# A DeltaNet recurrence with block-diagonal operands, weight buffers taken in turn, and one transition that adds its first half on VectorE

## The chip, the cores and the metric

The kernel runs on one core of a Trainium2 chip. The metric is the device time of one execution in microseconds (us); the time given for a kernel is the median over several executions.

A core has a matrix engine (TensorE; in the profile PE for the matrix products and PEld for the loading of their weights), a vector engine (VectorE, DVE), an activation engine (ScalarE, ACT), GpSimd (POOL), SyncE (SP), which here only issues transfers, and DMA engines. The engines run their own instruction queues in order and wait for each other through semaphores. SBUF holds tiles of 128 partitions; matrix products land in PSUM, of which this kernel makes eight buffers of 128x512 fp32: four named `pb` and four named `pd`.

## The reference

The kernel computes one layer of an encoder on a sequence of 512 positions with 16 learned positions ahead of it (528 in all) and 1024 channels:

```
h = h + 0.5 * post(swiglu_1(pre(h)))
h = h +       post(mixer(pre(h)))
h = h + 0.5 * post(swiglu_2(pre(h)))
```

`pre` and `post` are RMS norms. The mixer sums three gated branches and projects the sum with `w_out`. The branch that matters here is a gated delta rule with four heads of 128 channels, run once forward and once backward over the sequence in chunks of 64 positions:

```
def step(S, xs):                          # one chunk of one head and direction
    attn_n, u_n, w_n, qd_n, kd_n, gl_n = xs
    v_new = u_n - w_n @ S
    o = qd_n @ S + attn_n @ v_new
    S = S * gl_n[..., None, None] + jnp.swapaxes(kd_n, -1, -2) @ v_new
    return S, o
```

`t` (the inverse of a triangular 64x64 matrix) is folded into `u` and `w`; in the kernel it is applied to the difference instead.

## The kernel before, in words

**Weights.** All large products are made in fp32 accuracy from fp32r pieces: every weight block of 128 columns is brought by a DMA into `ws` (or `wf` in the FFNs), cast to fp32r by ScalarE (`wh`), and VectorE subtracts the cast from the original (`wl`). Three products, `wh` with the high and the low part of the data and `wl` with the high part, make one result. `load()` (lines 230 to 241) does this for a unit of one block, `pair_load()` (line 595 on) for the FFNs, where four blocks give seven combined ones. `wh` and `wl` live in the pool `wp`, which has 5 buffers for each, so a cast waits until TensorE has read the last of the block whose buffer it takes.

**Stages.** FFN 1 (to about 365 us), the transition `edge()` to the mixer, the mixer (to about 890 us; the output projection `w_out` makes up its end), the second `edge()`, FFN 2 and the output. TensorE's instructions stand in the order of the program text. The instructions of the other engines are placed by a scheduler with priorities: `AHEAD` puts loads 150 steps forward, `URGENT` evictions 450.

**The recurrence.** `dn_core` is a generator, run twice (two heads each time, each with a forward and a backward chain). It runs as a side program: whenever TensorE has worked for about `SC` = 1.8 us by the kernel's own count, `tick()` puts the next small group of products between those of the projections. A step s of 8 has three such groups. In the first, `kq` meets the state `Sst` (line 1446), and VectorE makes `vp` from the result (line 1450). In the second, `Z` (it shares the buffer `EZ`, and the profile shows that name) meets `vp` (line 1462), and ScalarE scales the result by `beta` into a second `vp` (line 1465; `v1` in the text). In the third, the decayed keys (`kd`, in the profile `sub`) and `at` meet `v1` (lines 1470 and 1473), and VectorE updates the state and the output `O`. A chunk has 64 positions, so the four products of `Z` and of `at` are 64x64, in the upper or lower half of the 128 partitions: at each step the forward chain is in one half and the backward chain in the other. The last step has no state to update, so its third group has `at` alone. An fp32 product shows as two PE records.

**The transitions.** In `edge()`, the last products of the stage before are accumulated for m = 0 to 7 in two halves of the columns. In the first edge, the sum of the earlier chunks (`y`) is copied into PSUM by ScalarE ahead of the products (line 355), which then add to it; the result is squared for the norm (lines 337 and 340) and copied back into `y` (line 343). VectorE sums the squares in `acc` (line 341). TensorE sums `acc` over the partitions (`stat`), and from the root VectorE and ScalarE make the new `h` and its pieces `x` block by block (`step`, lines 414 to 421), for which the first products of the next stage wait. In the second edge, the last three blocks of `w_out` make the tail, and the first blocks of FFN 2's weights are loaded.

Of the kernel before, what the change touches and what calls it, by code (L numbers as in the profile page):

```python
# [8 lines left out]
F32 = mybir.dt.float32  # L9
# [150 lines left out]
class K:  # L160
    def __init__(self, tc, A, ctx):
        self.tc, self.nc, self.A = tc, tc.nc, A
        self.n = 0
        self.sides = []
        self.T = Tensor(tc.nc)
# [4 lines left out]
        self.wp = e(tc.tile_pool(name="wp", bufs=5))  # L170
# [58 lines left out]
    def load(self, src, nk=KD, to=None):  # L229
# [100 lines left out]
    def leave_y(self, ya, m, ps, gain=None, table=KD - 2):  # L330
# [3 lines left out]
        for i, p in ps:  # L334
            w = acc[i].shape[1]
            if m == 0:
                ACT.activation(acc[i], p, AF.Square)
            else:
                sq = self.t(self.tp, "sy", [P, HN], F32, 1)[:, :w]
                ACT.activation(sq, p, AF.Square)  # L340
                V.tensor_tensor(acc[i], acc[i], sq, op=ALU.add)
            if gain is None:
# [19 lines left out]
    def start(self, xT, gpre, srcs):  # L362
# [8 lines left out]
               self.t(self.wp, "wl", [P, KD, P], F32R)) for i in range(len(srcs))]  # L371
        pieces = [slice(0, 1), slice(1, 2), slice(2, 4), slice(4, 6), slice(6, 8)]
# [30 lines left out]
    def edge(self, C, hT, ya, gpost, gpre, tail, switch, nxt, keep=None):  # L403
# [144 lines left out]
    def open_ffn(self):  # L548
        ctx = ExitStack()
        self.gp = ctx.enter_context(self.tc.tile_pool(name=self.uid("gp"), bufs=1))  # L550
        return ctx
# [44 lines left out]
    def pair_load(self, w1, w2):  # L596
# [4 lines left out]
        with self.tc.high_priority(AHEAD2):  # L601
# [7 lines left out]
            def put(f, a, b, w=KD, tag="w", pool=self.wp, bufs=None):  # L609
                h = self.t(pool, tag + "h", [P, w, P], F32R, bufs)  # L610
                l = self.t(pool, tag + "l", [P, w, P], F32R, bufs)
# [11 lines left out]
            put(fd, 4, None, 4, "w4", self.gp, 2)  # L623
# [242 lines left out]
    def mixer(self, pre, hT):  # L866
# [80 lines left out]
        def ready():  # L947
# [4 lines left out]
            mm = self.dctx.enter_context(self.tc.tile_pool(name="mm", bufs=1))  # L952
            return self.t(mm, "mh", [P, KD, S], F32R), self.t(mm, "ml", [P, KD, S], F32R)
# [13 lines left out]
        def tail():  # L967
            ws = [(m, self.load(A["wout"][m])) for m in range(KD - NT, KD)]
# [304 lines left out]
    def dn_core(self, st, slack):  # L1273
# [14 lines left out]
        at = self.t(dp, "at", B4)  # L1288
# [24 lines left out]
        for j in range(2):  # L1313
# [8 lines left out]
            for d in range(2):  # L1322
                V.tensor_tensor(A_[:, 2 * j + d], A_[:, 2 * j + d], b[:, :, 0], op=ALU.mult)
                V.tensor_tensor(at[:, 2 * j + d], E[:, 2 * j + d], b[:, :, 1], op=ALU.mult)
# [109 lines left out]
        yield SC  # L1434
        for s in range(8):
# [8 lines left out]
            vt = self.t(dp, "vp", [P, 4, P], F32, 2)  # L1444
# [3 lines left out]
            for j, d, hd, c, t, hf, X, Y, has in info:  # L1448
                if has:
                    V.scalar_tensor_tensor(vt[X, hd], b[X, hd * P:(hd + 1) * P], neg_eg[X, hd, t:t + 1], vn[X, j, t],  # L1450
                                           op0=ALU.mult, op1=ALU.add)
            for j, d, hd, c, t, hf, X, Y, has in info:
# [8 lines left out]
            for j, d, hd, c, t, hf, X, Y, has in info:  # L1461
                T.matmul(b[X, hd * P:(hd + 1) * P], Z[X, hd, t], vt[X, hd] if has else vn[X, j, t], start=True, stop=True)
            v1 = self.t(dp, "vp", [P, 4, P], F32, 2)
            for j, d, hd, c, t, hf, X, Y, has in info:
                ACT.activation(v1[X, hd], b[X, hd * P:(hd + 1) * P], AF.Copy, scale=beta[X, hd, t:t + 1])
            yield SC
            b = self.dnp()
            if s < 7:
                bS = [self.dnp(), self.dnp()]
                for j, d, hd, c, t, hf, X, Y, has in info:  # L1470
                    T.matmul(bS[d][:, j * P:(j + 1) * P], kd[X, (s // 2) % 2, hd], v1[X, hd], start=True, stop=True)
            for j, d, hd, c, t, hf, X, Y, has in info:
                T.matmul(b[X, hd * P:(hd + 1) * P], at[X, hd, t], v1[X, hd], start=True, stop=True)
# [139 lines left out]
```

## Time and profile before

| | |
|---|---|
| time, median of 3 runs | 1278.52 us (1276.74 to 1278.81) |
| time of the profiled execution | 1280.05 us |
| its span, first to last instruction | 1278.2 us |
| mean granted TensorE clock | 0.998 |
| busy: TensorE, VectorE, ScalarE | 1260.2, 943.3, 616.9 us |

1.85 us of the profiled execution lie outside its span. A row of the timeline gives start, length, engine, line, operation, output <- inputs, shape and count; in brackets stands how long the engine was idle before it and for whom. Rows of PE have lengths that are modelled, so what a product costs is read from one start to the next. Rows of the waits give the sum, the number of times and the longest. Rows of the windows give, for each engine, busy us and the number of instructions, and then the TensorE clock, the share of the DMA engines and GB/s.

### The profile page before, as it was taken

The page shows a single profiled execution, that of the slowest core. Times are in us where ns is not written, and L with a number is a line of the kernel's source. Part 1 is how long each engine was busy: PE and PEld are TensorE (multiplying, and loading weights), DVE is VectorE, ACT ScalarE, POOL GpSimd, SP SyncE. Part 2 cuts the span into 40 slices and gives each one's busy share as a digit, 9 for nine tenths or more (in the row PEclk, how much of TensorE's full clock was granted, in tenths as well). Part 3 has the DMA queues.
Part 4 walks back from the last instruction along what each step waited for, and adds up shares of the span by engine and source line. Part 5 has one row for each costly group of instructions (what it writes and reads, how often), then busy time and mean ns, then how long its engine had stood idle before and what let it go on. Part 6 is the DMA issues. An engine that isn't in the chain of part 4 may idle for free.

```text
span 1278.2 us, 23021 instructions
## 1 busy us (share of the span) xinstructions
PE 1260.2 (99%) x9111; PEld 1155.5 (90%) x9111; DVE 943.3 (74%) x1883; ACT 616.9 (48%) x1201; POOL 13.5 (1%) x28
## 2 busy tenths in 40 slices
PE   9999999999989999999999999999999999999998
PEld 9999999999989988778998777887988999999997
DVE  7978777766568779768799678554779887777654
ACT  7665444434386452344643534334566644444436
POOL 0000000000000000000000000000200000000000
PEclk9999999999999999999999999999999999999999
DMA  7243333321254222422221313235423433333213
GB/s 245 74 143 106 99 99 99 98 96 59 83 187 149 84 78 68 110 77 68 84 67 59 78 48 91 82 94 179 161 87 94 146 100 100 100 100 95 79 50 132
DMA packets 70207, 129.27 MB, mean 101 GB/s; under 512 B 15820, under 2 KB 24140, under 8 KB 70100
## 3 DMA queue, kind: packets, MB, share of 16 engines
q1 hardware_dynamic: 64244, 124.14, 31.1%
q10 hardware_dynamic: 5088, 1.57, 0.5%
q0 software_dynamic: 768, 2.10, 0.4%
q8 instruction: 71, 1.16, 0.4%
q14 instruction: 36, 0.29, 0.1%
HBM read 120.41 MB, written 7.37 MB: 100 GB/s over the span
## 4 chain that ended last, share of the span: by engine, by line
PE 82%; DVE 10%; DMA 2%; ACT 2%; issue 2%; SPq 1%; DVEq 0%; ACTq 0%
PE pb L153 52%; PE pd L153 29%; PE pd L157 1%; DVE wl L245 1%; DMA wf<-in_wi 1%; DVE wl L240 1%; DVE s L414 1%; DVE x L421 1%; DVE acc L312 1%; DVE h L416 1%; DMA ws<-in_wab 1%; ACT wh L239 0%; DVE h L568 0%; DMA h<-in_xT 0%; DMA ws<-in_wout 0%
## 5 line engine op out<-in xcount | busy, mean ns | idle before, releaser
L153 PE MATMUL pb<-x,wh 128*128 128x264 f32 (+3 forms) x1584 | 353.9, 327 | 4.3 <-DVE x L421 1.8
L153 PEld LDWEIGHTS pb<-x,wh 128*128 128x128 f32 x1584 | 247.0, 189 | 33.0 <-issue 4.2
L153 PE MATMUL pb<-x,wl 128*128 128x264 f32 (+3 forms) x792 | 220.4, 323 | 0.0
L153 PE MATMUL pb<-gh,h 128*128 128x264 f32 (+2 forms) x816 | 191.3, 320 | 3.1 <-ACT pb L355 3.1
L153 PE MATMUL pd<-x,wh 128*128 128x264 f32 (+2 forms) x1040 | 192.1, 284 | 0.0
L239 ACT CAST wh<-ws 128x1024 fp32r<-128x1024 f32 (+1 forms) x110 | 105.1, 956 | 170.7 <-PE pb L153 145.7
L244 ACT CAST wh<-wf 128x1024 fp32r<-128x1024 f32 x108 | 113.5, 1051 | 149.2 <-PE pd L153 119.7
L245 DVE TENSOR_TENSOR wl<-wf,wh 128x1024 fp32r<-128x1024 f32 x108 | 131.8, 1222 | 43.4 <-ACT wh L244 42.5
L153 PEld LDWEIGHTS pd<-x,wh 128*128 128x128 f32 x1040 | 160.0, 188 | 1.7
L240 DVE TENSOR_TENSOR wl<-ws,wh 128x1024 fp32r<-128x1024 f32 (+1 forms) x110 | 121.1, 1102 | 37.9 <-ACT wh L239 37.6
L153 PEld LDWEIGHTS pb<-x,wl 128*128 128x128 f32 x792 | 134.6, 188 | 12.4 <-DVE wl L384 0.2
L153 PEld LDWEIGHTS pb<-gh,h 128*128 128x128 f32 x816 | 132.0, 189 | 13.6 <-ACT pb L355 3.7
L153 PE MATMUL pd<-x,wl 128*128 128x264 f32 (+2 forms) x520 | 143.8, 284 | 0.0
L153 PE MATMUL pb<-gl,h 128*128 128x264 f32 (+2 forms) x456 | 123.7, 314 | 0.0
L153 PEld LDWEIGHTS pd<-x,wl 128*128 128x128 f32 x520 | 96.2, 188 | 0.4
L153 PEld LDWEIGHTS pb<-gl,h 128*128 128x128 f32 x456 | 78.3, 189 | 4.3
L153 PE MATMUL pd<-h,wh 128*128 128x264 f32 (+1 forms) x294 | 82.1, 282 | 0.0
L153 PE MATMUL pd<-l,wh 128*128 128x264 f32 (+1 forms) x288 | 81.5, 283 | 0.0
L153 PE MATMUL pd<-h,wl 128*128 128x264 f32 (+1 forms) x288 | 81.4, 283 | 0.0
L698 DVE TENSOR_TENSOR y<-y,pb 128x264 f32<-128x264 f32 (+1 forms) x128 | 48.6, 420 | 30.8 <-PE pb L153 30.8
L239 ACT CAST h<-ws 128x1024 fp32r<-128x1024 f32 (+1 forms) x40 | 38.5, 968 | 60.3 <-PE pb L153 50.5
L153 PE MATMUL pb<-y,wh 128*128 128x512 f32 x192 | 61.3, 400 | 0.0
(325 smaller groups left out, 2295.4 us busy)
## 6 DMA issues: line engine op xcount, KB each, us to landing
wf<-in_wi SPq DMA_DIRECT2D x144, 256.0 KB, 2.6
ws<-in_wo SPq DMA_DIRECT2D x64, 256.0 KB, 3.0
ws<-in_win SPq DMA_DIRECT2D x32, 512.0 KB, 3.6
ws<-in_wg SPq DMA_DIRECT2D x24, 512.0 KB, 3.5
ws<-in_wi SPq DMA_DIRECT2D x13, 512.0 KB, 3.8
ws<-in_wo SPq DMA_DIRECT2D x32, 192.0 KB, 2.4
ws<-in_wout SPq DMA_DIRECT2D x8, 512.0 KB, 3.6
h<-in_xT SPq DMA_DIRECT2D x10, 264.0 KB, 5.3
```

The source lines that it names most:

```text
L153: return self.e.matmul(out, lhsT, rhs, **kw)
L157: return self.e.transpose(*a)
L239: nc.scalar.copy(h[:, :n], st[:, :n])
L240: nc.vector.tensor_tensor(l[:, :n], st[:, :n], h[:, :n].bitcast(F32), op=ALU.subtract)
L244: self.nc.scalar.copy(h, src)
L245: self.nc.vector.tensor_tensor(l, src, h.bitcast(F32), op=ALU.subtract)
L312: V.tensor_tensor(acc, acc, sq, op=ALU.add)
L414: V.scalar_tensor_tensor(t, ya[0][i][:, k, :W], self.gains[:, gpost, k:k + 1], r[:, c], op0=ALU.mult, op1=ALU.mult)
L416: V.tensor_tensor(hT[:, k, c], hT[:, k, c], t, op=ALU.add)
L421: V.scalar_tensor_tensor(x[1][:, k, c], hT[:, k, c], g, x[0][:, k, c].bitcast(F32), op0=ALU.mult, op1=ALU.subtract)
L698: V.tensor_tensor(y, y, p, op=ALU.add)
```

## The change

Three parts.

1. In `dn_core`, `Z` is copied by ScalarE into a block-diagonal tile `ZB` (two copies a step, one for each direction, a step ahead), and `at` is made as a block-diagonal tile by VectorE (eight products into 64 partitions instead of four into 128). GpSimd clears both once a round. A step's two chains of one head stand in the two halves of one tile, so that `Z` and `at` take two 128x128 products each instead of four of 64x64, and ScalarE scales two 128x128 blocks instead of four of 64x128.
2. `wp` has 4 buffers. In the FFNs every fifth block has a buffer of its own (`wh5`, `wl5`), and the last three blocks of `w_out` get theirs in the pool `mm` (`th`, `tl`).
3. In the first edge, the first half of the columns isn't preloaded into PSUM; VectorE adds the result to `y`, and the square is taken from `y`. The second half is as before.

```diff
-        self.wp = e(tc.tile_pool(name="wp", bufs=5))
+        self.wp = e(tc.tile_pool(name="wp", bufs=4))
...
+    def wtile(self, tag):
+
+        n = self.turn[tag] = (self.turn.get(tag, 0) + 1) % 5
+        if self.five and n == 0:
+            return self.t(self.gp, tag + "5", [P, KD, P], F32R)
+        return self.t(self.wp, tag, [P, KD, P], F32R)
...
-            h, l = to or (self.t(self.wp, "wh", [P, KD, P], F32R), self.t(self.wp, "wl", [P, KD, P], F32R))
+            h, l = to or (self.wtile("wh"), self.wtile("wl"))
...
         for i, p in ps:
             w = acc[i].shape[1]
+            if onto:
+                V.tensor_tensor(y[i][:, m, :w], y[i][:, m, :w], p, op=ALU.add)
+                p = y[i][:, m, :w]
...
-            if gain is None:
+            if onto:
+                pass
+            elif gain is None:
                 ACT.copy(y[i][:, m, :w], p)
...
+        self.five = False
         tiles, tx, tc, more = tail()
...
-            self.evict_y(ya, t[0], [(0, self.part(t, tx, tc[0], W, more and ya[0][0]))], table=tiles[1][0] if more else -1)
+            self.evict_y(ya, t[0], [(0, self.part(t, tx, tc[0], W))], table=tiles[1][0] if more else -1, onto=bool(more))
...
-            ws = [(m, self.load(A["wout"][m])) for m in range(KD - NT, KD)]
+            ws = [(m, self.load(A["wout"][m], to=[self.t(self.mm2, i, [P, KD, P], F32R, NT) for i in ("th", "tl")]))
+                  for m in range(KD - NT, KD)]
...
-                V.tensor_tensor(at[:, 2 * j + d], E[:, 2 * j + d], b[:, :, 1], op=ALU.mult)
+                for hf in range(2):
+                    X = slice(hf * 64, hf * 64 + 64)
+                    V.tensor_tensor(at[X, j, hf::2, X] if d == 0 else at[X, j, 1 - hf::2, X], E[X, 2 * j + d][:, ::1 - 2 * d],
+                                    b[X, ::1 - 2 * d, 1], op=ALU.mult)
...
+        def blocks(s):
+            for d in range(2):
+                c = s if d == 0 else 7 - s
+                X = slice((c % 2) * 64, (c % 2) * 64 + 64)
+                ACT.copy(ZB[X, s % 2, :, X], Z[X, d::2, c // 2])
...
-            for j, d, hd, c, t, hf, X, Y, has in info:
-                T.matmul(b[X, hd * P:(hd + 1) * P], Z[X, hd, t], vt[X, hd] if has else vn[X, j, t], start=True, stop=True)
-            v1 = self.t(dp, "vp", [P, 4, P], F32, 2)
-            for j, d, hd, c, t, hf, X, Y, has in info:
-                ACT.activation(v1[X, hd], b[X, hd * P:(hd + 1) * P], AF.Copy, scale=beta[X, hd, t:t + 1])
+            for j in range(2):
+                T.matmul(b[:, j * P:(j + 1) * P], ZB[:, s % 2, j], vt[:, j], start=True, stop=True)
+            v1 = self.t(dp, "vp", [P, 2, P], F32, 2)
+            for j in range(2):
+                ACT.activation(v1[:, j], b[:, j * P:(j + 1) * P], AF.Copy, scale=bB[:, j, s:s + 1])
+            if s < 7:
+                blocks(s + 1)
...
-            for j, d, hd, c, t, hf, X, Y, has in info:
-                T.matmul(b[X, hd * P:(hd + 1) * P], at[X, hd, t], v1[X, hd], start=True, stop=True)
+            for j in range(2):
+                T.matmul(b[:, j * P:(j + 1) * P], at[:, j, s], v1[:, j], start=True, stop=True)
```

On TensorE, the third group of a step stood like this before, between two products of the projection (`wl`, `wh`):

```order
L153 MATMUL pb_8468<-x_4209,wl_8464 128x512
L153 MATMUL pd_8509<-vp_8494,sub_8449 128x128
L153 MATMUL pd_8510<-vp_8494,sub_8449 128x128
L153 MATMUL pd_8509<-vp_8494,sub_8449 128x128
L153 MATMUL pd_8510<-vp_8494,sub_8449 128x128
L153 MATMUL pd_8508<-vp_8494,at_7594 64x128 x4
L153 MATMUL pb_8468<-x_4209,wh_8463 128x512
```

and stands like this now, at the same place:

```order
L153 MATMUL pb_8453<-x_4209,wl_8449 128x512
L153 MATMUL pd_8505<-vp_8490,sub_8434 128x128
L153 MATMUL pd_8506<-vp_8490,sub_8434 128x128
L153 MATMUL pd_8505<-vp_8490,sub_8434 128x128
L153 MATMUL pd_8506<-vp_8490,sub_8434 128x128
L153 MATMUL pd_8504<-vp_8490,at_7572 128x128 x2
L153 MATMUL pb_8453<-x_4209,wh_8448 128x512
```

The four products with `at` (64 rows by 128) became two of 128 by 128; nothing else moved there, and the group with `Z` in the middle of the step changes in the same way (`EZ` x4 to `ZB` x2).

On ScalarE, at the start of a step of the second round, before (`O` and `vp` are the step's output and scaled blocks, `wh` casts are projection weights, `t` is the gate of a branch):

```order
L1456 ACTIVATE O_8411<-pd_8472,eg_5363 64x128 x2
L1465 ACTIVATE vp_8494<-pd_8489,be_5093 64x128 x4
L239 CAST wh_8758<-ws_8757 128x512
L1486 COPY O_8411<-pd_8508 64x128
L979 ACTIVATE t_1134_8530<-t_1134_8530 128x512
L1486 COPY O_8411<-pd_8508 64x128
L239 CAST wh_8802<-ws_8801 128x1024
L1456 ACTIVATE O_8411<-pd_8546,eg_5363 64x128 x4
L1465 ACTIVATE vp_8583<-pd_8578,be_5093 64x128 x4
L239 CAST wh_8879<-ws_8878 128x512
```

and now:

```order
L1495 ACTIVATE O_8396<-pd_8468,eg_5355 64x128 x2
L1504 ACTIVATE vp_8490<-pd_8487,bB_8457 128x128 x2
L1470 COPY ZB_7573<-EZ_8123 64x2x64 x2
L247 CAST wh_8669<-ws_8668 128x1024
L1527 COPY O_8396<-pd_8504 64x128
L996 ACTIVATE t_1138_8524<-t_1138_8524 128x512
L1527 COPY O_8396<-pd_8504 64x128
L247 CAST wh_8742<-ws_8741 128x512
L1495 ACTIVATE O_8396<-pd_8540,eg_5355 64x128 x4
L1504 ACTIVATE vp_8575<-pd_8572,bB_8457 128x128 x2
L1470 COPY ZB_7573<-EZ_8123 64x2x64 x2
L247 CAST wh_8784<-ws_8783 128x1024
```

The weights' casts stand one load further back against the steps (the 128x512 cast that stood behind the step's `vp` now stands behind the next `O` copies), `vp` is two instructions, and two copies into `ZB` stand behind it.

On ScalarE, in the second edge, before (`sy` and `y` are the evictions of the `w_out` blocks, `x` the first pieces for FFN 2):

```order
L298 ACTIVATE rt_10017<-pd_10014,eps_82 128x2
L239 CAST wh_10162<-ws_10161 128x1024
L340 ACTIVATE sy_10029<-pb_9998 128x256
L343 COPY y_9693<-pb_9998 128x256
L295 COPY r_9889<-pd_10037 128x256
L239 CAST wh_10168<-ws_10167 128x1024
L340 ACTIVATE sy_10080<-pb_10033 128x256
L343 COPY y_9693<-pb_10033 128x256
L420 ACTIVATE x_9890<-h_9690,gains_77 128x256 x2
L308 ACTIVATE acc_10427<-h_9690 128x256
L311 ACTIVATE sx_10429<-h_9690 128x256
L239 CAST wh_10480<-ws_10479 128x1024
```

and in the changed kernel the casts of these blocks (numbers 10126 and 10132, ahead of the table load for the root) stand among the evictions of the blocks ahead of the tail:

```order
L247 CAST wh_10126<-ws_10125 128x1024
L351 ACTIVATE sy_9843<-pb_9812 128x256
L356 COPY y_9656<-pb_9812 128x256
L247 CAST wh_10132<-ws_10131 128x1024
L351 ACTIVATE sy_9847<-pb_9812 128x256
L356 COPY y_9657<-pb_9812 128x256
L360 ACT_TABLE_LOAD
L360 ACTIVATE junk_81<-acc_9658 128x1
```

while at the place of the rows of before there is now:

```order
L306 ACTIVATE rt_9981<-pd_9978,eps_82 128x2
L351 ACTIVATE sy_9993<-pb_9962 128x256
L356 COPY y_9657<-pb_9962 128x256
L303 COPY r_9853<-pd_10001 128x256
L434 ACTIVATE x_9854<-h_9654,gains_77 128x256 x2
L316 ACTIVATE acc_10391<-h_9654 128x256
L351 ACTIVATE sy_10044<-pb_9997 128x256
L356 COPY y_9657<-pb_9997 128x256
L319 ACTIVATE sx_10393<-h_9654 128x256
L434 ACTIVATE x_9854<-h_9654,gains_77 128x256
```

The two casts moved from the stretch in which `x` is made to the one before it; the subtractions that follow them on VectorE moved with them.

More of the change, by code (lines that the diff above doesn't have):

```diff
@@ L164, in __init__ @@
         self.sides = []
+        self.turn, self.five = {}, False
         self.T = Tensor(tc.nc)
@@ L328, in evict_y, with leave_y @@
             self.leave_y(*a, **kw)
-    def leave_y(self, ya, m, ps, gain=None, table=KD - 2):
+    def leave_y(self, ya, m, ps, gain=None, table=KD - 2, onto=False):
         y, acc = ya
@@ L371, in start @@
                self.t(self.wp, "wl", [P, KD, P], F32R)) for i in range(len(srcs))]
+        self.turn = {n: len(srcs) for n in ('wh', 'wl')}
         pieces = [slice(0, 1), slice(1, 2), slice(2, 4), slice(4, 6), slice(6, 8)]
@@ L550, in open_ffn @@
         self.gp = ctx.enter_context(self.tc.tile_pool(name=self.uid("gp"), bufs=1))
+        self.turn, self.five = {}, True
         return ctx
@@ L607, in pair_load, with put @@
             nc.sync.dma_start(fc[:, hi], w2[:, hi])
-            def put(f, a, b, w=KD, tag="w", pool=self.wp, bufs=None):
-                h = self.t(pool, tag + "h", [P, w, P], F32R, bufs)
-                l = self.t(pool, tag + "l", [P, w, P], F32R, bufs)
+            def put(f, a, b, w=KD, new=self.wtile):
+                h, l = new(f"w{'4' if w < KD else ''}h"), new(f"w{'4' if w < KD else ''}l")
                 self.split(h, l, f[:, :w])
@@ L622, in pair_load @@
             V.tensor_tensor(fd[:, lo], fb[:, hi], fb[:, lo], op=ALU.add)
-            put(fd, 4, None, 4, "w4", self.gp, 2)
+            put(fd, 4, None, 4, lambda n: self.t(self.gp, n, [P, 4, P], F32R, 2))
         return out
@@ L1287, in dn_core @@
         E = self.t(dp, "EZ", B4)
-        at = self.t(dp, "at", B4)
+        at = self.t(dp, "at", [P, 2, 8, P])
+        ZB = self.t(dp, "ZB", [P, 2, 2, P])
+        nc.gpsimd.memset(at, 0.0)
+        nc.gpsimd.memset(ZB, 0.0)
         B2 = [32, 2, 32]
@@ L1434, in dn_core @@
         yield SC
+        bB = self.t(dp, "bB", [P, 2, 8])
+        for j, d in chains:
+            for hf in range(2):
+                X = slice(hf * 64, hf * 64 + 64)
+                V.tensor_copy(bB[X, j, (hf if d == 0 else 1 - hf)::2], beta[X, 2 * j + d, 0:4][:, ::1 - 2 * d])
+        def blocks(s):
[3 more added lines that the diff above has]
+                ACT.copy(ZB[X, s % 2, :, X], Z[X, d::2, c // 2])
+        blocks(0)
         for s in range(8):
@@ L1470, in dn_core @@
                 for j, d, hd, c, t, hf, X, Y, has in info:
-                    T.matmul(bS[d][:, j * P:(j + 1) * P], kd[X, (s // 2) % 2, hd], v1[X, hd], start=True, stop=True)
-            for j, d, hd, c, t, hf, X, Y, has in info:
-                T.matmul(b[X, hd * P:(hd + 1) * P], at[X, hd, t], v1[X, hd], start=True, stop=True)
+                    T.matmul(bS[d][:, j * P:(j + 1) * P], kd[X, (s // 2) % 2, hd], v1[X, j], start=True, stop=True)
+            for j in range(2):
+                T.matmul(b[:, j * P:(j + 1) * P], at[:, j, s], v1[:, j], start=True, stop=True)
             if s < 7:
```

9 lines of the change are left out of this document (6 added, 3 removed).

## The prediction

> **What bounds the kernel now.** The page comes first: how much of the span TensorE works, and the chain of work that ended last.
>
> ```profile
> span 1278.2 us, 23021 instructions
> PE 1260.2 (99%) x9111; PEld 1155.5 (90%) x9111; DVE 943.3 (74%) x1883; ACT 616.9 (48%) x1201; POOL 13.5 (1%) x28
> PE 82%; DVE 10%; DMA 2%; ACT 2%; issue 2%; SPq 1%; DVEq 0%; ACTq 0%
> ```
>
> TensorE is busy for 99% of the span, and 82% of the chain is its own. A change gains where it shortens TensorE's stream or takes a wait out of it. The waits of PE, and of its weight loads, are short:
>
> ```profile
> PE pb L153 <- ACT pb L355: 3.1, 3, 2.6
> PE pb L153 <- DVE x L421: 1.8, 4, 0.7
> PE pb L153 <- ACT x L420: 1.2, 1, 1.2
> ...
> PEld pd L153 <- ACT vp L1465: 2.3, 6, 0.5
> PEld pd L153 <- DVE vp L1450: 1.8, 6, 0.4
> ```
>
> The first row is the first transition (PSUM preloads), the next two are mostly the second (`x`), and the last two are the recurrence. So three places are to be worked out, one after the other.
>
> **The recurrence: fewer products.** A busy PE hides what a product costs; the timeline's starts show it. Two groups of round 1:
>
> ```profile
> 542.11 0.39 PE L153 MATMUL pb<-y,wl 128*128 128x512 f32 x1
> 542.34 0.61 PE L153 MATMUL pd<-Sst,kq 128*128 128x128 f32 x4
> ...
> 543.25 0.39 PE L153 MATMUL pb<-y,wl 128*128 128x512 f32 x1
> ...
> 562.75 0.39 PE L153 MATMUL pb<-x,wl 128*128 128x512 f32 x1
> ...
> 563.45 0.39 PE L153 MATMUL pb<-x,wl 128*128 128x512 f32 x1
> 563.76 0.65 PE L153 MATMUL pd<-vp,EZ 64*64 64x128 f32 x8
> ...
> 564.92 0.40 PE L153 MATMUL pb<-y,wl 128*128 128x512 f32 x1
> ```
>
> From one `wl` to the next is 0.70 us without a group (562.75 to 563.45). With the group of `Z` between them it is 1.47 (563.45 to 564.92), so eight 64x64 records cost 0.77. With four records of 128x128, which is just what two full fp32 products leave, it is 1.14 (542.11 to 543.25), so they cost 0.44. The change puts the second shape in place of the first: 0.33 us a group. The groups are counted by:
>
> ```profile
> L153 PE MATMUL pd<-vp,EZ 64*64 64x128 f32 x120 | 11.2, 283 | 0.0
> L153 PE MATMUL pd<-vp,at 64*64 64x128 f32 x128 | 10.7, 282 | 0.0
> ...
> 616.06 0.65 PE L153 MATMUL pd<-vp,at 64*64 64x128 f32 x8
> ```
>
> `Z` has 8 steps in each of 2 rounds, 16 groups (120 records and 8 that read `vn`): 16 x 0.33 = **5.3 us**. I bound it by 4.5 and 5.5, since the shape was seen only twice. `at` has 128 records in 16 groups. Two of them, in the last step of each round, stand alone with the same 0.65 us as `Z`: 2 x 0.33 = **0.7 us**. The other 14 follow the products with `sub`:
>
> ```profile
> 771.81 0.39 PE L153 MATMUL pb<-x,wl 128*128 128x512 f32 x1
> 772.13 0.71 PE L153 MATMUL pd<-vp,sub 64*128 64x128 f32 x8
> 772.77 0.65 PE L153 MATMUL pd<-vp,at 64*64 64x128 f32 x8
> 773.93 0.39 PE L153 MATMUL pb<-x,wl 128*128 128x512 f32 x1
> ```
>
> Both together cost 773.93 - 771.81 - 0.70 = 1.42 us. No row has full products behind `sub`, so I bound the gain from both sides: 0 if all that is saved at the border to the projection is paid at the border to `sub`, and 0.33 if nothing is. My value keeps the entry (0.09, from 772.13 - 771.81 - 0.23, the start to start of a 512-column record, a third of 0.70), `sub` (0.64), the 0.44 of the full pair, and 0.10 for a border behind `sub`, as large as the entry: 1.27, so 0.15 a step, 14 x 0.15 = **2.1 us** (0 to 4.6).
>
> The Trainium skill ("TensorEngine Tiling (Array Packing)", Key Properties) says that a change of the tiling mode drains TensorE. By that, the alone-standing groups lose both of their drains, and `at` behind `sub` loses one of two, which lies between my ends; 0.64 to the first `at` against 0.44 for as many full records agrees.
>
> **The recurrence: ScalarE and VectorE.** ScalarE's work is the same in sum: a step loses two `vp` instructions of 0.38 (1.51 / 4 below) and gains two copies into `ZB`, of the size of a 0.38 copy (`pb<-y` below). But the copies stand behind `vp`, and what TensorE waits for is two instructions, not four. Where it is late now:
>
> ```profile
> 566.38 1.51 ACT L1465 ACTIVATE vp<-pd,be 64x128 f32<-64x128 f32 x4
> 566.78 1.65 PE L153 MATMUL pd<-vp,sub 64*128 64x128 f32 x8
> 568.36 0.65 PE L153 MATMUL pd<-vp,at 64*64 64x128 f32 x8
> ```
>
> `sub` to `at` takes 1.58 there, against 0.64 undisturbed, since each `sub` waits for its `vp`. With two instructions the last is ready at 566.38 + 0.76, not at 567.89. The starts of all groups give 1.8 us lost so in the run (1.08 in this group with its entry); I expect **1.3 us** of it back. Bounds are 2.6 (the 0.78 that a late VectorE costs one group of `Z` goes too) and -2, if the casts of weights, which have moved against the steps, fall ahead of `vp` instead:
>
> ```profile
> ACT wh L239 <- PE pb L153: 145.7, 54, 5.5
> ```
>
> A cast waits in ScalarE's queue for TensorE to free its buffer, 145.7 us in all, and `vp` and the output copies stand behind it. With four buffers, a cast at the same place would wait one load longer; the order shows each cast one load further back against the steps instead, so it waits for the same product as before. What that costs is lead: a block is ready one load later. TensorE waits for no `wh` or `wl` of the mixer in the list above, so there is lead to give; if it didn't suffice, those waits would appear.
>
> The one loss that I can place is the making of `at`, eight VectorE instructions a round instead of four:
>
> ```profile
> L1324 DVE TENSOR_TENSOR at<-EZ,pd x8: 401/406/411, 465.8 to 656.3; 128x256 f32<-128x256 f32 x8
> 467.62 0.28 PE L157 MATMUL pd<-ident,um 128*32 128x128 f32 x1 [0.68 <-ACT vn L1212]
> ```
>
> Each has the same 256 elements a partition, so it takes the same 0.41 us, and the PSUM buffer that the next products take comes free two of these later. In round 1 TensorE waits there already, so it is on the path: **-1.0 us** for two rounds (0 to -1.5). GpSimd's clearing, VectorE's copies of `vn` and of `beta` come stages ahead of use, or where VectorE waits for TensorE anyway; without that cover I would put them at one late group, 1 us.
>
> **The first transition.**
>
> ```profile
> 360.73 0.39 ACT L340 ACTIVATE sy<-pb 128x264 f32<-128x264 f32 x1
> 361.02 0.37 ACT L343 COPY y<-pb 128x264 f32<-128x264 f32 x1
> 361.42 0.38 ACT L355 COPY pb<-y 128x264 f32<-128x264 f32 x1
> ...
> 363.19 0.28 PE L153 MATMUL pb<-gh,l 128*128 128x264 f32 x1
> ...
> 363.57 1.04 ACT L239 CAST wh<-ws 128x1024 fp32r<-128x1024 f32 x1 [1.17 <-DMA ws<-in_wab]
> ...
> 366.07 0.39 PE L153 MATMUL pb<-gh,h 128*128 128x264 f32 x1 [2.60 <-ACT pb L355]
> ...
> 367.00:370.00 3.00, 3.00 (x18) 3.00 (x17) 0.80 (x4) 2.45 (x6) 0.00 (x0) 0.56 0.51 167
> 370.00:373.00 3.00, 3.00 (x23) 3.00 (x23) 2.47 (x5) 2.07 (x7) 0.00 (x0) 0.87 0.28 40
> ```
>
> ScalarE spends 1.14 us a tile on three instructions. The preload of the second half stands behind a cast that waits 1.17 us for its DMA, and TensorE stands still for 3.1 us (2.6 + 0.5). Behind that the granted clock is 0.56 for 3 us and 0.87 for 3 us: 3 x 0.44 + 3 x 0.13 = 1.7 us more. The change leaves ScalarE one instruction a tile in the first half, and the preloads of the second half go early and together, ahead of that cast. So all 4.8 us can go. I give back 1.4: VectorE now does 8 adds more, the sum of squares is ready a little later, and the cast (1.04) now stands ahead of the root. **3.4 us** (1 to 4.8).
>
> **The second transition.**
>
> ```profile
> 905.29 1.23 DVE L240 TENSOR_TENSOR wl<-ws,wh 128x1024 fp32r<-128x1024 f32 x1 [1.67 <-ACT wh L239]
> ...
> 909.36 1.22 DVE L240 TENSOR_TENSOR wl<-ws,wh 128x1024 fp32r<-128x1024 f32 x1
> ...
> 910.00:920.00 10.00, 9.14 (x74) 8.67 (x73) 9.94 (x25) 5.67 (x14) 3.23 (x6) 1.00 0.81 274
> 920.00:930.00 10.00, 10.00 (x88) 10.00 (x87) 10.00 (x27) 5.96 (x15) 3.24 (x6) 1.00 0.40 136
> ```
>
> VectorE is full from 910 to 930 us and makes `x`, for which TensorE waits (the 1.8 and 1.2 us of the waits above, some of it in the first transition). Two `wl` subtractions of 1.22 us are in that chain. The order puts both ahead of the tail, where TensorE has work and VectorE has room, so the last `x` comes 2 x 1.22 = 2.4 us earlier: **2.4 us** (0, if transfers or another `wl` take the place, to 4.1, if the whole wait goes). In the FFNs TensorE doesn't wait, and `wp` with its fifth buffer gives the same distances: 0.
>
> **Sum.** 5.3 + 0.7 + 2.1 + 1.3 - 1.0 + 3.4 + 2.4 = 14.2 us. Against the profiled execution's 1280.05 that is 1265.8; the median shown is 1278.52, 1.5 below it, and from there it is **1264.3 us**.
>
> **Rivals.**
> - *The transitions give it back.* The full VectorE is what both depend on, and it gets 8 adds. Then only the recurrence's 8.4 us stay, plus 1 of the first transition: 1269. For it: DVE at 10.00 of 10; against: the removed subtractions are in that very chain.
> - *The narrow products were as good as full ones.* Eight 64x64 records start in pairs, so the array time of both shapes is alike; if the 0.33 is not the shape's but the neighbours', the recurrence keeps 0, and 5.8 from the transitions less 1.0 leaves 1273.7. Against: 0.44 was measured in two groups of the same shape in the same stream. The Trainium skill ("TensorE: Matmul & The Clock Gate", Part 3) says that tiles of the array run beside each other at a few ns distance, which speaks for this rival; the 0.65 us for eight records agrees with it, the entry and exit do not.
> - *All waits go*, with the clock's loss: 5.5 + 0.7 + 3 + 2.6 - 0.5 + 4.8 + 4.1 = 20.2, so 1258.3.
> - *Slower: four buffers hold ScalarE's queue.* Place: 14 steps with `sub`. If a cast of 1.05 us and a gate of 0.63 come between the group of `Z` and `vp`, each step waits 1.68 us: 23.5 lost against 12.9 won elsewhere, 1289. It decides from 1.1 us a step on. For it: 145.7 us of casts that wait; against: the order puts `vp` ahead of the next cast in each step I compared.
> - *It doesn't do what it says:* the order shows it does on TensorE; only lost lead could cancel it, near 1278.
>
> **Chances.** Forecast (1261 to 1267) 0.52; transitions give back 0.18; narrow as good 0.07; all waits go 0.12; no gain 0.05; slower 0.06. The range takes in the first two and most of the fourth: **1258 to 1271**. 0.2% is 2.6 us, about what a measurement of this kernel can tell from no change. Faster by more: 0.52 + 0.18 + 0.07 + 0.12 = 0.89; within: 0.05; slower: 0.06.
>
> **What would show it.** The groups of `ZB` should cost 0.44 us from `wl` to `wl` (0.77 says the shape gained nothing), the third groups 1.27, `sub` should no longer be spread out near the eighth of a round, no PE wait should stand on `pb` L355's successor and the clock should stay at 1.00 after the first transition, and VectorE should reach its last `x` some 2.4 us earlier against TensorE's first products. A row "PEld pd <- ACT vp" above 5 us, or PE waiting for `wh` or `wl` in the mixer, would make the prediction wrong.

## The result, and the profile after

The changed kernel takes **1267.30 us** (median of 4 runs, 1266.60 to 1267.55) against 1278.66 for the kernel before (4 runs, 1276.74 to 1279.74): a ratio of 0.9912, 95% interval 0.9900 to 0.9925. The forecast was 1264.3 with a range of 1258 to 1271, so 11.4 us were won where 14.2 were expected. The profiled execution of the changed kernel took 1267.55 us, 12.5 less than that of before.

The head of the page, to be read against the same rows of before:

```profile
span 1265.5 us, 22787 instructions
PE 1248.3 (99%) x8983; PEld 1154.1 (91%) x8983; DVE 955.5 (75%) x1919; ACT 607.4 (48%) x1185; POOL 17.9 (1%) x32
PE 87%; DVE 7%; ACT 3%; DMA 2%; issue 1%; SPq 0%; DVEq 0%; ACTq 0%
```

TensorE has 128 records less and works 11.9 us less, and its share of the chain that ended last rose from 82% to 87%.

**Where the time went.** TensorE's instructions stand in one order, so nearly every product outside the recurrence has a counterpart in each kernel of this study. The table gives, at six places of the program (named by the time at which the kernel before is there), how much earlier or later than before the same products start in the profiled execution of each kernel; the last column is the time from the end of round 1 to the start of round 2 alone (the column at 716 less the one at 618, before rounding).

| kernel | 410: behind the first edge | 618: behind round 1 | 716: ahead of round 2 | 867: behind round 2 | 945: in FFN 2 | 1260 | between the rounds |
|---|---|---|---|---|---|---|---|
| the change | -4.2 | -8.1 | -3.5 | -8.2 | -11.8 | -12.7 | **+4.6** |
| the change, again | -4.0 | -7.9 | -3.3 | -8.0 | -11.5 | -11.7 | +4.6 |
| e2, edge only | -3.4 | -3.4 | -3.4 | -3.5 | -4.3 | -4.9 | 0.0 |
| e3, buffers only | -0.4 | +0.3 | +0.3 | -0.4 | -3.9 | -4.8 | 0.0 |
| e4, `at` by GpSimd | -4.2 | -8.1 | -5.4 | -10.1 | -13.6 | -14.5 | +2.7 |
| e5, `Z` only | -5.2 | -8.0 | -7.6 | -11.3 | -14.8 | -15.7 | +0.4 |
| e6, two `bB` | -4.3 | -8.2 | -6.0 | -10.7 | -14.2 | -15.0 | +2.1 |
| e7, cleared once | -4.2 | -8.2 | -5.3 | -10.0 | -13.6 | -14.5 | +2.9 |
| e8, both | -4.8 | -8.7 | -6.5 | -11.2 | -14.8 | -15.7 | +2.2 |
| e9, both and ScalarE | -4.0 | -7.9 | -7.7 | -12.4 | -15.9 | -16.7 | +0.3 |
| e11, tail in `wp` | -4.5 | -8.4 | -4.2 | -8.9 | -8.3 | -9.0 | +4.2 |

The change wins 4.2 us by the end of the first edge, 3.9 and 4.7 in the two rounds and 3.6 in the second edge, and **loses 4.6 between the rounds**. That stretch is the surprise: for the making of `at`, in both rounds together, the prediction had set aside 1.0.

The profiled execution of before is 1.4 us above its median, and a part of what the table shows behind round 2 is that execution's own: e2 touches nothing there, and yet it wins 0.8 from 867 to 945 and 0.6 behind it. One execution also differs from the next by up to about 1 us at a single place: e5 has the first edge of the change and is 5.2 ahead behind it where the change is 4.2. This is why the pair of profiles differs by more than the medians.

**The groups of the recurrence.** The timeline of TensorE around one group with `ZB`, and around one third group:

```profile
558.93 0.40 PE L153 MATMUL pb<-x,wl 128*128 128x512 f32 x1
559.16 0.61 PE L153 MATMUL pd<-vp,ZB 128*128 128x128 f32 x4
559.53 0.71 PE L153 MATMUL pb<-y,wh 128*128 128x512 f32 x2
560.08 0.39 PE L153 MATMUL pb<-y,wl 128*128 128x512 f32 x1
...
774.02 0.39 PE L153 MATMUL pb<-x,wl 128*128 128x512 f32 x1
774.34 0.71 PE L153 MATMUL pd<-vp,sub 64*128 64x128 f32 x8
774.98 0.71 PE L153 MATMUL pd<-vp,at 128*128 128x128 f32 x4
775.45 0.71 PE L153 MATMUL pb<-x,wh 128*128 128x512 f32 x2
776.00 0.39 PE L153 MATMUL pb<-x,wl 128*128 128x512 f32 x1
```

The first is 560.08 - 558.93 - 0.70 = 0.45 us, where 0.77 stood before. The second is 776.00 - 774.02 - 0.70 = 1.28, where 1.42 stood: 0.64 to the first `at` as before, and full products behind it. The groups with `at` alone cost 0.45 too. These are the sizes forecast (0.44 and 1.27).

The lateness did not go away, it changed its place. The timelines of VectorE and of TensorE in the second step of round 1:

```profile
547.61 1.22 DVE L248 TENSOR_TENSOR wl<-ws,wh 128x1024 fp32r<-128x1024 f32 x1 [0.16 <-ACT wh L247]
548.87 0.71 DVE L1487 SCALAR_TENSOR_TENSOR vp<-pd,neg_eg,vn 64x128 f32<-64x128 f32 x2
```
```profile
549.63 0.49 PE L153 MATMUL pd<-vp,ZB 128*128 128x128 f32 x2
550.38 0.49 PE L153 MATMUL pd<-vp,ZB 128*128 128x128 f32 x2 [0.26 <-DVE vp L1487]
```

Here a subtraction of weights stands ahead of `vp` in VectorE's queue, and the two halves of the group start 0.75 apart. At 753.15 it is a smaller subtraction and the addition of a branch's product (751.18 and 751.78) that stand ahead of `vp`. These two groups cost 0.75 and 0.72 more than the others, three groups 0.12 to 0.17 more, and the third group at 561.95 only 0.22 where before it was 1.08. Together that is some 2.1 us of lateness, against 1.8 and 0.78 before.

**The first edge.** The windows that stand where the clock was 0.56 and 0.87 before, and two rows of the waits:

```profile
363.70:366.70 3.00, 2.42 (x22) 2.21 (x21) 1.69 (x4) 2.29 (x7) 0.00 (x0) 1.00 0.02 7
366.70:369.70 3.00, 3.00 (x27) 3.00 (x26) 2.44 (x7) 2.93 (x10) 0.00 (x0) 1.00 0.56 175
```
```profile
PE pd L153 <- DVE rt L307: 0.6, 1, 0.6
PE pb L153 <- ACT pb L368: 0.2, 1, 0.2
```

The wait for the preloads is 0.2 us instead of 3.1, and the granted clock stays at 1.00. A wait of 0.6 us for the root (`rt`, at 366.28) is new there.

**Between the rounds.** The waits of TensorE from 620 us on (to 690 in before, to 680 after), first of the kernel before, then of the changed one:

```profile
PE pd L153 <- ACT zfold L1038: 1.1, 2, 0.6
PE pd L153 <- DVE t L1030: 0.2, 1, 0.2
```
```profile
PE pd L153 <- ACT zfold L1055: 1.8, 3, 0.6
PE pd L157 <- ACT sq L1274: 0.9, 1, 0.9
PE pd L153 <- ACT t L1064: 0.5, 1, 0.5
PE pd L153 <- DVE t L1047: 0.4, 1, 0.4
PE pd L153 <- DVE t L1044: 0.3, 1, 0.3
```

There are 3.9 us of waits where there were 1.3. These rows don't hold the whole loss, since the ends of PE's rows are modelled. From one start to the next, against the kernel before, 1.1 us are lost at 628.40 (the products with `kn`, which wait for `sq`), 1.9 from 649 to 652 (`zfold` and `t`), 1.0 from 669 to 670 and 0.6 from 705 to 706. The waits name ScalarE or VectorE and `zfold`, `t` and `sq`, none of which the change touches: the cause stands further back. Two candidates can be seen in VectorE's timeline. The first is at the end of round 1 (GpSimd's row stands last; the idle time in its bracket is its own):

```profile
608.61 2.94 DVE L1464 COPY bB<-be 64x4 f32<-64x4 f32 x7
611.58 0.29 DVE L1525 TENSOR_TENSOR O<-O,pd 64x128 f32<-64x128 f32 x1
...
608.83 1.81 POOL L1308 MEMSET at<- 128x2048 f32 x1 [2.01 <-PE pd L153]
```

These are the copies of `beta` into `bB` for round 2. `bB` has one buffer, so they can only be made once round 1's last `vp` has read it, and in VectorE's queue they stand ahead of the last additions to `O`. VectorE isn't idle before them (no bracket): they cost by running at this place. One of these tiny copies ran beside GpSimd's clearing of `at`; the view of the tile `bB` shows how long it took:

```profile
L1464 DVE COPY bB<-be x16: 96/167/1870, 420.9 to 611.4; 64x4 f32<-64x4 f32 x16
```

The median is 0.167 us, this one took 1.87. The last products with `at` start at 608.16, and the first of their `O` additions at 611.58, 3.4 us later (before it was 0.7: 616.79 less 616.06). Until the additions have read them, the results of these products keep their PSUM buffer.

The second is the making of `at` itself:

```profile
648.34 0.40 DVE L1344 TENSOR_TENSOR A<-A,pd 128x256 f32<-128x256 f32 x1
648.66 0.84 DVE L1347 TENSOR_TENSOR at<-EZ,pd 64x256 f32<-64x256 f32 x2
...
652.26 0.84 DVE L1347 TENSOR_TENSOR at<-EZ,pd 64x256 f32<-64x256 f32 x2
```

Eight products into 64 partitions take 0.42 us each, as long as the four into 128 did, and the whole series lasts from 648.34 to 653.1, 4.8 us. In the kernel before it was 2.7, with the first and the last row:

```profile
653.97 0.40 DVE L1323 TENSOR_TENSOR A<-A,pd 128x256 f32<-128x256 f32 x1
...
656.29 0.40 DVE L1324 TENSOR_TENSOR at<-EZ,pd 128x256 f32<-128x256 f32 x1
```

In the changed kernel one row of the weight loads names the series itself:

```profile
650.75 0.74 PEld L153 LDWEIGHTS pd<-const,t 128*128 128x128 f32 x6 [0.32 <-DVE at L1347]
```

These products belong to another stage and read nothing of `at`. They start right behind the fourth of its eight products (649.86 + 0.84 = 650.70), the last to read the first PSUM buffer of the series: so they wait for a buffer.

The prediction had this in round 1, at 467 us; there it cost nothing (the shift is the same -4.2 from 410 us to the start of the first round's steps, and TensorE's wait for `vn` is 0.7 us in both kernels). It costs in round 2, where another stage wants the same PSUM buffers.

### The profile page after: what moved, and what is told of

Its sections match the earlier page's. It is cut to its first block, busy times and chain, and to the rows that moved or that the text cites. A ratio compares the mean times of both kernels' runs of the same rounds, so it can differ in the third digit from the quotient of the medians.

```text
span 1265.5 us, 22787 instructions
## 1 busy us (share of the span) xinstructions
PE 1248.3 (99%) x8983; PEld 1154.1 (91%) x8983; DVE 955.5 (75%) x1919; ACT 607.4 (48%) x1185; POOL 17.9 (1%) x32
## 4 chain that ended last, share of the span: by engine, by line
PE 87%; DVE 7%; ACT 3%; DMA 2%; issue 1%; SPq 0%; DVEq 0%; ACTq 0%
PE pb L153 53%; PE pd L153 32%; PE pd L157 1%; DVE wl L248 1%; DMA h<-in_xT 1%; DMA ws<-in_wab 1%; DVE x L435 1%; DVE s L428 0%; DVE h L430 0%; DVE vp L1487 0%; DMA Ad<-s 0%; ACT y L358 0%; DVE t L556 0%; DVE acc L320 0%; ACT wh L247 0%
## 5 line engine op out<-in xcount | busy, mean ns | idle before, releaser
L247 ACT CAST wh<-ws 128x1024 fp32r<-128x1024 f32 (+1 forms) x107 | 101.8, 953 | 149.3 <-PE pb L153 114.2
L248 DVE TENSOR_TENSOR wl<-ws,wh 128x1024 fp32r<-128x1024 f32 (+1 forms) x107 | 117.5, 1099 | 23.8 <-ACT wh L247 23.4
```

Source lines behind the costliest of these rows:

```text
L247: nc.scalar.copy(h[:, :n], st[:, :n])
L248: nc.vector.tensor_tensor(l[:, :n], st[:, :n], h[:, :n].bitcast(F32), op=ALU.subtract)
```

## The experiments

The theory: the edge and the buffers win by themselves as forecast, and the 4.6 us are lost to VectorE's queue, by the copies into `bB` and by the products of `at`. The rivals: the buffers (a cast one load later) lose it; or the 128x128 products with `ZB` push something back; or it is one cause alone.

### The first edge alone (e2)

The kernel before with part 3 of the change: the first half added to `y` by VectorE, no preload for it.

```diff
-            self.evict_y(ya, t[0], [(0, self.part(t, tx, tc[0], W, more and ya[0][0]))], table=tiles[1][0] if more else -1)
+            self.evict_y(ya, t[0], [(0, self.part(t, tx, tc[0], W))], table=tiles[1][0] if more else -1, onto=bool(more))
```

> The kernel before with the first edge's change alone (first half of the columns added by VectorE). Theory, from the starts of the matrix products in the two traces: the first edge gives 4.3 us and nothing is given back behind it, so 1274.3 us. Rival 1, the recorded term of 3.4: 1275.3. Rival 2, what is won early is lost again in the mixer, where VectorE sets the pace: 1277 or more.

Measured: 1274.44 us (11 runs, 1273.81 to 1276.48) against 1277.99 (21 runs), ratio 0.9974 (0.9966 to 0.9983), so 3.55 us are won. In the table it is all won in that edge (-3.4 at 410 us), and nothing is lost between the rounds. That is the recorded term of 3.4 (rival 1) rather than the 4.3 of the theory: the time itself is close to the theory's 1274.3, but the kernel before took 0.7 less here than in the first runs.

### The buffers alone (e3)

The kernel before with part 2: four buffers in `wp`, a fifth in the FFNs, `th` and `tl` for the tail.

```diff
-        self.wp = e(tc.tile_pool(name="wp", bufs=5))
+        self.wp = e(tc.tile_pool(name="wp", bufs=4))
...
-            ws = [(m, self.load(A["wout"][m])) for m in range(KD - NT, KD)]
+            ws = [(m, self.load(A["wout"][m], to=[self.t(self.mm2, i, [P, KD, P], F32R, NT) for i in ("th", "tl")]))
+                  for m in range(KD - NT, KD)]
```

> The kernel before with the buffers' change alone (4 buffers and a fifth in the FFNs, th and tl for the tail). Theory: 2.5 us at the second edge and 1 us at the output projection, and the later casts in the mixer cost nothing: 1275.2 us. Rival: the casts that stand one load further back put VectorE's subtractions ahead of vp and of the preparation of round 2, and the waits of 4.6 us that the trace of the change shows between the two rounds are theirs: 1278 to 1280, and PE waits between 610 and 720 us.

Measured: 1274.49 us (11 runs), ratio 0.9973 (0.9964 to 0.9983), 3.5 us won. That agrees with the theory's 3.5, and the table shows it behind round 2 (3.5 from 867 to 945, of which 0.8 may be that of the execution of before). It shows 0.0 between the rounds, so the rival that blames the buffers falls. It also shows what four buffers do to the steps: round 1 loses 0.7 and round 2 wins as much. One such step, in VectorE's timeline and TensorE's:

```profile
752.54 1.23 DVE L248 TENSOR_TENSOR wl<-ws,wh 128x1024 fp32r<-128x1024 f32 x1 [0.58 <-ACT wh L247]
```
```profile
752.54 1.28 PE L153 MATMUL pd<-vp,sub 64*128 64x128 f32 x8
753.75 0.65 PE L153 MATMUL pd<-vp,at 64*64 64x128 f32 x8
```

The subtraction falls into the group with `sub`, which lasts 1.21 us to the first `at` instead of 0.64. So where a subtraction meets a step is set by the buffers, with the old recurrence as with the new one.

Both parts together win 7.0. The recurrence by itself was not run: with five buffers in `wp` its larger tiles need more SBUF than is left. If the parts add up, it is worth 11.4 - 7.0 = 4.4 us with the loss between the rounds, which agrees with the table: 8.6 won in the two rounds, 4.6 lost between them.

### `at` by four products, spread by GpSimd (e4)

The changed kernel; the products of `at` are made in place in `EZ`, four of 128 partitions as before, and GpSimd copies the halves to their places.

```diff
+                V.tensor_tensor(E[:, 2 * j + d], E[:, 2 * j + d], b[:, :, 1], op=ALU.mult)
                 for hf in range(2):
                     X = slice(hf * 64, hf * 64 + 64)
-                    V.tensor_tensor(at[X, j, hf::2, X] if d == 0 else at[X, j, 1 - hf::2, X], E[X, 2 * j + d][:, ::1 - 2 * d],
-                                    b[X, ::1 - 2 * d, 1], op=ALU.mult)
+                    nc.gpsimd.tensor_copy(at[X, j, hf::2, X] if d == 0 else at[X, j, 1 - hf::2, X], E[X, 2 * j + d][:, ::1 - 2 * d])
```

> The changed kernel, but at is again made by four VectorE products of 128x256 a round, and GpSimd copies it into the block-diagonal tile. Theory: the eight products of 64x256 hold the PSUM buffers and VectorE 1.7 us longer a round, and that is the wait of 1.9 us at the Fourier products behind them in round 2, and a part of the 1.5 us that follows: 1264.0 to 1265.4 us, with those waits gone. Rival: TensorE, which is 8 us earlier there, only meets a VectorE that was always this slow; then 1266.5 to 1267.3 and the waits stay. Second rival: GpSimd's copies keep VectorE from SBUF and nothing is won: 1267.3.

Measured: 1265.98 us (1265.76 to 1268.82), ratio 0.9913 (0.9899 to 0.9927). By the times this can't be told from the change (0.9912), and it lies between the theory's range and the rival's, in neither. The table is finer: between the rounds 2.7 are lost instead of 4.6. So VectorE's second set of products accounts for some 1.9 us, and it isn't the only cause: the wait of the products with `kn` for `sq` stays as it was.

### `Z` block-diagonal, `at` as before (e5)

The changed kernel, with `at` made, stored and used as before: four products, nothing cleared, four 64x64 products a step.

```diff
-            for j in range(2):
-                T.matmul(b[:, j * P:(j + 1) * P], at[:, j, s], v1[:, j], start=True, stop=True)
+            for j, d, hd, c, t, hf, X, Y, has in info:
+                T.matmul(b[X, j * P:(j + 1) * P], at[X, hd, t], v1[X, j], start=True, stop=True)
```

> The changed kernel with at as before (four 64x64 products, made by four VectorE instructions); Z stays block-diagonal. Theory: 14 x 0.14 + 2 x 0.33 = 2.6 us of at's gain are lost and 1.9 to 3.3 us of its making are won back: 1266.6 to 1268.0 us. Rival, the making costs nothing of its own: 1269.9.

Measured: 1266.15 us (1265.19 to 1266.46), ratio 0.9908 (0.9895 to 0.9922), a little better than expected. Between the rounds only 0.4 is lost, so the products with `ZB` are not the cause and that rival falls too: with `at` as before, 4.2 of the 4.6 are gone. In return the rounds win 2.9 and 3.6 instead of 3.9 and 4.7, which is 2.1 for `at` less. As a whole, the block-diagonal `at` of the change is worth nothing: it loses between the rounds at least what it wins inside them, and the times with and without it are the same within their intervals.

### The change again (c)

The changed kernel a second time, on the chip on which e6, e8 and e9 ran, so that these stand beside it.

> The changed kernel once more, beside the three that follow on the same chip: 1267.3 us by its first runs; 1266.5 if the chip is the one of the last four runs, where the kernel before took 1278.0.

Measured: 1267.58 us (1266.85 to 1269.05) against 1277.84 (9 runs), ratio 0.9918 (0.9903 to 0.9932). The loss between the rounds is 4.6 again.

### Two buffers for `bB` (e6)

The changed kernel; the copies of round 2 no longer wait for round 1's last `vp`.

```diff
-        bB = self.t(dp, "bB", [P, 2, 8])
+        bB = self.t(dp, "bB", [P, 2, 8], F32, 2)
```

> The changed kernel with two buffers for bB, so that round 2's eight copies no longer wait in VectorE's queue for round 1's last vp. Theory: in the change these copies and the clearing of at by GpSimd, which holds one of them 1.87 us, stand ahead of round 1's last output adds and set VectorE back by 2.7 us; that is the wait of 1.06 us at the key products (628.40) and about 0.6 us of the waits behind it: 1.7 us less than the change, with the output adds 0.8 us behind their products. Rival: TensorE is simply ahead of a preparation that VectorE paces, so the wait stays whatever stands ahead: 0 to 0.3 us less.

Measured: 1264.96 us (1264.20 to 1265.89), ratio 0.9896 (0.9880 to 0.9912), 2.6 us below the change on this chip, more than the 1.7 expected. VectorE's timeline at the end of round 1 now has the first `O` addition right behind the products:

```profile
608.76 0.29 DVE L1525 TENSOR_TENSOR O<-O,pd 64x128 f32<-64x128 f32 x1 [0.27 <-PE pd L153]
```

It starts at 608.76 instead of 611.58, the wait for `sq` is gone, and the loss between the rounds falls from 4.6 to 2.1. So the copies into `bB` ahead of the additions are one cause, the first of the two candidates, with 2.5 us.

### The tiles cleared once (e7)

The changed kernel, with one buffer for `bB`; but `at` and `ZB` are made once, and cleared once ahead of round 1. The places outside the diagonal blocks are never written, so they stay zero in round 2.

```diff
-        at = self.t(dp, "at", [P, 2, 8, P])
-        ZB = self.t(dp, "ZB", [P, 2, 2, P])
-        nc.gpsimd.memset(at, 0.0)
-        nc.gpsimd.memset(ZB, 0.0)
+        if r == 0:
+            self.blk = self.t(dp, "at", [P, 2, 8, P]), self.t(dp, "ZB", [P, 2, 2, P])
+            for z in self.blk:
+                nc.gpsimd.memset(z, 0.0)
+        at, ZB = self.blk
```

> The changed kernel with at and ZB cleared once for both rounds; round 2's copies into bB still wait in VectorE's queue for round 1's last vp. Theory: without the clearing the eight copies take 1.2 us and not 2.9, so of the 2.3 us that the copies out of the way gave, the share of the held copy, 1.2 to 1.7 us, comes back here: 1265.8 to 1266.4 us, and the wait at the key products falls from 1.06 us to nothing. Rival: it is the place in the queue alone that counts, not the clearing: 1267.3 us and the wait stays.

Measured: 1265.59 us (1264.64 to 1266.55) against 1277.61 (9 runs), ratio 0.9902 (0.9887 to 0.9917). The same place in VectorE's timeline:

```profile
608.62 1.24 DVE L1465 COPY bB<-be 64x4 f32<-64x4 f32 x7
609.89 0.29 DVE L1526 TENSOR_TENSOR O<-O,pd 64x128 f32<-64x128 f32 x1
```

The seven copies take 1.24 us instead of 2.94, so it was the clearing that held one of them; the wait for `sq` is gone here too, and the loss between the rounds falls by 1.7, to 2.9. Of the 2.5 us of `bB`'s copies, then, about 1.7 are this one held copy, and 0.8 the copies themselves. In e5, where the copies stand in the queue as well and nothing holds them, all that is lost is 0.4; so the 0.8 hangs on what comes behind them, which was not followed further.

### Both (e8)

e6 and e7 together.

> As e6_bb_two, and at and ZB are cleared once for both rounds, since every block is written over in place. Theory: the clearing only hurt through the copy that it held, so no more than 0.3 us less than e6_bb_two. Rival: it holds whatever VectorE does at 608 us, then 1 us or more less than e6_bb_two.

Measured: 1265.73 us (1264.72 to 1266.16), ratio 0.9900 (0.9885 to 0.9916), the same as e6 within what can be told. Once nothing stands ahead of the `O` additions, the clearing costs nothing; 2.2 stay lost, as in e6.

### Both, and `at` spread by ScalarE (e9)

e8, with the products of `at` made as in e4 and spread by ScalarE.

```diff
+                    ACT.copy(at[X, j, hf::2, X] if d == 0 else at[X, j, 1 - hf::2, X], E[X, 2 * j + d][:, ::1 - 2 * d])
```

> As e8_both, and at is made by four VectorE products of 128x256 a round, which ScalarE copies into the block-diagonal tile (eight copies of 64x256). Theory: with the copies ahead of the output adds and the longer making both gone, none of the 4.6 us between the rounds is lost: 4 us less than the change, 1262.5 to 1263.5 us, if ScalarE has room for 8 x 0.38 us there. Rival: the four products still leave VectorE behind a TensorE that is 8 us earlier: 2 us less than the change.

Measured: **1263.14 us** (1262.49 to 1265.60), ratio 0.9884 (0.9867 to 0.9901): 14.7 below the kernel before, 4.4 below the change on the same chip, faster than both. TensorE's timeline at the place where the change waits for `zfold` and `t`:

```profile
646.96 2.10 PE L153 MATMUL pd<-tabz,zfold 128*128 128x134 f32 x16
649.12 1.60 PE L153 MATMUL pd<-const,t 128*128 128x128 f32 x12
```

In the change these products come in four pieces with waits between:

```profile
649.45 1.18 PE L153 MATMUL pd<-tabz,zfold 128*128 128x134 f32 x8 [0.47 <-ACT t L1064]
...
652.31 0.94 PE L153 MATMUL pd<-const,t 128*128 128x128 f32 x6 [0.62 <-ACT zfold L1055]
```

The loss between the rounds is 0.3, and both rounds keep their 3.9 and 4.7. So the second cause (1.9 us from e8 to e9, as from the change to e4) and the first (2.5) add up to 4.4 of the 4.6.

### The tail of `w_out` in `wp` (e11)

The changed kernel, but the last three blocks of `w_out` take their buffers from `wp` in turn, with four now instead of five.

```diff
-            ws = [(m, self.load(A["wout"][m], to=[self.t(self.mm2, i, [P, KD, P], F32R, NT) for i in ("th", "tl")]))
-                  for m in range(KD - NT, KD)]
+            ws = [(m, self.load(A["wout"][m])) for m in range(KD - NT, KD)]
```

> The changed kernel with the last three blocks of w_out loaded into wp again (4 buffers). Theory: the second edge's 2.4 us come from th and tl alone, which let two casts and subtractions of FFN 2's weights go ahead of the tail; with four buffers a third one falls back into the stretch, so 2.4 to 3.6 us more than the change: 1269.7 to 1271 us. Rival: the second edge got shorter because TensorE arrives there 8 us earlier, or by the four buffers: 1267.3 us.

Measured: 1272.28 us (1271.18 to 1272.75), ratio 0.9953 (0.9941 to 0.9966), 4.7 above the change (c, on another chip); somewhat more than expected. The waits of TensorE:

```profile
PE pb L153 <- DVE x L435: 2.3, 4, 0.8
PE pb L153 <- ACT x L434: 2.0, 2, 1.3
```

(in the change 0.3 and 1.1), and, in VectorE's timeline, one of three subtractions that now stand among the instructions that make `x`, with the `x` behind it:

```profile
899.41 1.22 DVE L248 TENSOR_TENSOR wl<-ws,wh 128x1024 fp32r<-128x1024 f32 x1
900.54 0.88 DVE L435 SCALAR_TENSOR_TENSOR x<-h,gains,x 128x256 fp32r<-128x256 f32 x2
```

In the change two are made at 883.34 and 885.81, and one stays in the chain, at 905.16 (the kernel before had three there, at 905.29, 909.36 and 917.28):

```profile
883.34 1.23 DVE L248 TENSOR_TENSOR wl<-ws,wh 128x1024 fp32r<-128x1024 f32 x1 [0.95 <-ACT wh L247]
...
885.81 1.22 DVE L248 TENSOR_TENSOR wl<-ws,wh 128x1024 fp32r<-128x1024 f32 x1 [0.91 <-ACT wh L247]
```

From 867 to 945 us the change wins 3.6, e11 loses 0.6. So the second edge isn't won without the buffers `th` and `tl`, which let the subtractions go ahead of the chain. That TensorE comes earlier is not needed for it: e3 wins 3.5 there with TensorE at the old time.

## Why the prediction was right, and where it was not

1. *The groups with `Z` (5.3) and with `at` alone (0.7): right.* 0.45 instead of 0.77 each. The rival "the narrow products were as good" (1273.7) is out.
2. *`at` behind `sub` (2.1): right.* 1.28 instead of 1.42, against 1.27 forecast. It fits that only one of the two borders goes: the time from the first `sub` to the first `at` is 0.64 as before, and a group gains 0.14, where the groups that lose both borders gain 0.33.
3. *ScalarE and VectorE's lateness (1.3): too large.* The third group near the eighth of a round is no longer spread out, as forecast, but two groups with `ZB` are late in its place, where before one group with `Z` was (the 0.78). From 2.6 us of lateness (1.8 and the 0.78 that the text kept apart) 2.1 are left, so it is worth some 0.5. Points 1 to 3 make 8.6 us measured in the two rounds, 9.4 forecast.
4. *The making of `at` (-1.0, bounded by 0 and -1.5): **the step that failed**.* It lost 4.6 us. The duration was right (eight times 0.42 us), and two things were wrong. The place: in round 1, where the prediction put it on the path because TensorE waits there already, it costs nothing (that wait, for `vn`, is 0.7 us with four products and with eight), and in round 2 some 1.9 us, since the series holds a PSUM buffer for which another stage waits. And the cover of what was costed at nothing: "GpSimd's clearing, VectorE's copies of `vn` and of `beta` come stages ahead of use, or where VectorE waits for TensorE anyway". Ahead of use they do come, but the copies of `beta` have a buffer that round 1 still reads, so they can't be made before its last `vp`, and round 1's last `O` additions stand behind them in VectorE's queue; the clearing then holds one of them. That is 2.5 us. The text priced the loss of this cover at "one late group, 1 us"; it had looked at when the copies are needed and not at when they may be written, and what is queued behind them until then.
5. *The first transition (3.4, 1 to 4.8): right.* e2 alone wins 3.55. TensorE's wait for the preloads is 0.2 us, and the clock doesn't fall. Of the losses that it allowed for (1.4: the sum of squares later, the cast ahead of the root), a new wait of 0.6 us for the root is what the trace shows.
6. *The second transition (2.4, 0 to 4.1): right.* The pair of profiles shows 3.6; e2, with no change there, wins 0.8 of it too, so that much is put down to the one execution of before, and 2.7 is left. Of three subtractions in the chain two left it, the two that the prediction counted on. e11 shows that it hangs on the tail's own buffers, though not its size, since with four buffers in `wp` more subtractions fall into the chain than before.
7. *The rival of ScalarE's queue (1289)* did not come: in the mixer's rounds there is no wait of TensorE for `wh`, and "PEld pd <- ACT vp" is 1.3 us where 5 was the sign. e3 shows that the buffers do move where subtractions fall, with 0.7 us either way.
8. *The rival by which the transitions give it back (1269)* is out as well: e2 and e3 win 7.0 us without the recurrence. *All waits go* (1258.3) did not come either; e9, with three repairs, reaches 1263.1.

With 4.6 in place of 1.0 and the lateness at 0.5, the sum is 14.2 - 3.6 - 0.8 = 9.8, and the edges, which won 0.15 and 0.3 more than forecast, bring it to 10.3. Measured were 11.4, and the interval of the ratio, 9.6 to 12.8 us, holds both. So the forecast of 1264.3 was 3.0 us too low, mainly for one term. The measured 1267.3 lies just outside the band that the prediction called its forecast (1261 to 1267). The stated range holds it because it was drawn wide enough for a rival at 1269 that did not come, so that it is inside is in part luck; the mechanisms of points 1, 2, 5 and 6 are not.

## What to carry to other kernels

A copy costed at nothing because it comes ahead of its use can still hold up a queue: ask when its buffer may be written, and what stands behind it on its engine until then; a second buffer for sixteen numbers a partition was worth 2.6 us here. Splitting one instruction over halves of the partitions doubled its cost here (0.42 us for each half, 0.41 for the whole), and as it reads PSUM, that was paid by the stage that wanted the buffer next, not by the one in which it stands. And a block-diagonal operand paid best where it removed both of its borders to other products: `ZB` gained 0.33 us a group, `at` behind `sub` 0.14, which its making ate up until e9.

## What the runs showed of the hardware

A VectorE copy of 64x4 elements, 0.167 us in the median, took 1.87 us while GpSimd cleared 128x2048 elements (1.81 us), and ended with it: at 610.66, the clearing at 610.64. In e7, without that clearing, the longest of these sixteen copies takes 0.168 us. The Trainium skill ("SBUF — State Buffer", in the section "SBUF: two separate sides") says that VectorE and GpSimd share a pair of ports as an exclusive lock, which one instruction holds to its end while the other blocks, and it counts an fp32 copy inside SBUF among VectorE's instructions that take the pair. The 1.87 beside 1.81 agrees with it, though the copy's record starts 0.04 us ahead of the clearing's; that it is this lock, and not something else between the two engines, no run here shows.
